# A fused RWKV-7 and Conformer layer: loads of the Pool queue held back and spread over slots, first loads in the order of use, the bonus loaded at once behind the recurrence

## The chip, the cores and the metric

The kernel runs on one core of one Trainium2 chip. The metric is device time in microseconds of one execution, from the first to the last instruction with what lies around it; three runs of the kernel before took 1825.54, 1830.32 and 1831.36 us, median 1830.32 us. A second kind of number is the span of a profiled execution, from its first to its last instruction.

## The reference

One layer works on 256 tokens of width 4096. A pre-normed input goes through one input projection; its columns feed an RWKV-7 group (32 heads of 64) and a Conformer convolution group of 2048 channels; both are gated, joined, projected again, post-normed and added to the input. Cut to what matters here:

```python
h = rms_norm(x, norm_pre_g)
proj = einsum('btd,dc->btc', h, w_in)                 # 256 x 4096 x 14528
rwkv_in, g_rwkv, glu_v, glu_g, g_conv = split(proj)
xs = rwkv_in + (prev - rwkv_in) * mu_shift            # token shift
r, k, v, w_low, a_low = split(xs)
decay = exp(-exp(-softplus(-(w0 + tanh(w_low) @ w_lora_up)) - 0.5))
a = sigmoid(a0 + a_low @ a_lora_up)
kk = k * k_k; kk = kk / max(norm(kk), 1e-12)
k_h = k * (1 + (a - 1) * k_a)
# per head, S of 64 x 64, over 256 steps:
#   S = S diag(w_t) + (S (-kk_t)) (kk_t a_t)^T + v_t k_t^T ;  y_t = S r_t
y = rwkv7_recurrence(r, decay, k_h, v, kk, a)
y = group_norm(y) * lnx_g + lnx_b
bonus = sum(r * k_h * r_k, per head) * v
y_rwkv = (y + bonus) * silu(g_rwkv)
c = silu(layer_norm(causal_conv31(glu_v * sigmoid(glu_g)) + conv_b))
y_conv = (c @ w_pw2 + b_pw2) * silu(g_conv)
out = concat([y_rwkv, y_conv]) @ w_out                # 256 x 4096 x 4096
return x + rms_norm(out, norm_post_g)
```

## The kernel before

The three big products are cut into blocks of 512 columns and 128 rows of depth. Their weights come from HBM in tiles `wr` of two depth steps (512 KB), issued on the SP queue five tiles ahead (`load`, four buffers). ScalarE rounds each 128x512 half to a TensorE format (`wh`), VectorE writes the rest of the rounding (`wl`), and TensorE forms three products per half of the tokens: `wh,lh`, `wl,lh`, `wh,ll`. One depth step of one block is a slot; it is six matmuls of 512 columns. The loop over `slots` writes PE, DVE and ACT out by hand (`MANUAL`): in each slot the six matmuls, then `side.step()`, then the `wh` of four slots later (`HL`) and the `wl` of three slots later (`LL`). The first two blocks run interleaved.

All else is side work: generators in lanes, which `side.step()` moves on once per slot. A plain `yield` ends a lane's part of the slot; `yield 0` lets it go on as long as a running account of DVE and ACT work stays below that of PE. Since the three engines run in the order in which instructions were written, a side instruction that waits holds up the `wh`, `wl` or matmuls written behind it.

The side work that the change touches, for 8 units `u` of 4 heads, two quads `qd` of 4 units:

- `job_prep(u)` (lane 4) forms the operands of the recurrence in chunks of 32 steps: `c_ar`, `c_q`, `c_bkt`, `c_uv`, and stores them on the POOL queue into the DRAM tensor `rec_dr`; a part of `c_q` goes into `n_dr`, the bonus `c_bv` into `bv_dr`.
- `job_inv(pr)` (lane 3) inverts the triangular 32x32 matrices of two units: an identity is loaded into `t_x` (line 595), `n_dr` is loaded four times into `c_y`, to 32 partitions each (line 600), and 31 steps of two DVE instructions follow, the first of which reads both (`c_sq<-t_x,c_y`).
- `job_chain(qd)` (lane 2) runs the recurrence over 8 chunks. `fetch(c)` loads one chunk's operands, 1 MB, from `rec_dr` into `c_st` (two buffers). At the end it norms the result and, per unit, loads the bonus into `t_x` (line 741), waits six slots and adds.

POOL and SP are not in `MANUAL`. A scheduler orders their DMA issues and may place an issue earlier than the code has it, as far as its tile is free and its source is written. Nothing else waits for an issue: it starts when the POOL queue comes to it.

At the start, `x_load(0)` loads the first four rows of tiles of the transposed input into `c_ar` and, between them, the first two weight halves; `load(1)` to `load(4)` follow. `WARM` matmuls on a zero tile run meanwhile.

Of the kernel before, what the change touches and what calls it, by code (L numbers as in the profile page):

```python
# [9 lines left out]
F32 = mybir.dt.float32  # L10
# [7 lines left out]
P = 128  # L18
# [6 lines left out]
CH = 32  # L25
NCH = T // CH
BN = 512
KC = 2
COL = dict(r=0, k=2048, v=4096, low=6144, g=6336, gv=8384, gg=10432, gc=12480)
PT = 2  # L30
RL0 = (BN + 2 * LORA) // 2
WARM = 9
SLACK = 0.0
CREDIT = 1500.0
HI_LEAD, LO_LEAD = 4, 3
# [142 lines left out]
def hybrid(ctx: ExitStack, tc, a, out):  # L178
# [108 lines left out]
    def x_load(i):  # L287
        if i < 4:
            st["xc"] = rw["pool"].tile([P, 4, T + 1], F32, name=XTAG[i], bufs=1)
        elif i % 2 == 0:  # L290
            st["xc"] = rw["pool"].tile([P, 8, T + 1], F32, name="c_st", bufs=2)
        o = 4 * (i % 2) if i > 3 else 0
        t = st["xc"][:, o:o + 4, :]
        if i == 0:
            for k0, k1 in ((0, 1), (1, 2), (2, 4)):
                nc.sync.dma_start(out=t[:, k0:k1, :], in_=xT_v[:, k0:k1, :])
                if k0 < KC:
                    load(0, k0)
        else:
            nc.sync.dma_start(out=t, in_=xT_v[:, 4 * i:4 * i + 4, :])  # L300
        st["xr", i] = t
# [98 lines left out]

    def c3(x):
        return x[:, 0:512].rearrange("p (c t) -> p c t", t=CH)

    def crossed(out, in_):

# [21 lines left out]
    def job_prep(u):  # L427
# [87 lines left out]
                scale=par("k_a", u * 2 + q), bias=oka[:, u * 2 + q:u * 2 + q + 1])  # L515
        vec.tensor_tensor(out=ar4[:, :, 0::3], in0=e2(c3(rs)), in1=e2(pt_[:, :, 1:C1]), op=ALU.mult)
        yield 0
        vec.tensor_tensor(out=kkn, in0=kkn, in1=av, op=ALU.mult)
        yield 0
        for q in range(2):  # L520
# [31 lines left out]
                                in_=qs[y * CH:(y + 1) * CH, :, 1 - x::2, x * CH:(x + 1) * CH])  # L552
        rw[("n", u)] = True
        for h in range(2):
            nc.gpsimd.dma_start(out=rec_dr[qd, :, :, un, 0, h * 64:h * 64 + 64].rearrange("c p x -> p c x"), in_=ar[:, h * 8:h * 8 + 8, :])  # L555
            nc.gpsimd.dma_start(out=rec_dr[qd, :, :, un, 1, h * 64:h * 64 + 64].rearrange("c p x -> p c x"), in_=qs[:, h])

        bp = yield from head_sums(bq, "t_sw")
# [30 lines left out]
    def job_inv(pr):  # L589

        rp = rw["pool"]
        while ("n", 2 * pr + 1) not in rw or (pr > 1 and not rw.get(("done", pr // 2 - 1))):
            yield "wait"
        xi = rp.tile([P, 2, 8, CH], F32, name="t_x", bufs=1)
        nc.gpsimd.dma_start(out=xi.rearrange("p n l k -> p (n l k)"), in_=a["cst"][:, CS["eye"][0]:CS["eye"][1]])
        yield
        yield
        nt = rp.tile([P, 2, CH, CH], F32, name="c_y", bufs=1)
        for rho in range(4):
            nc.gpsimd.dma_start(out=nt[rho * 32:(rho + 1) * 32].rearrange("p n k j -> p n (k j)"),  # L600
                                in_=n_dr[2 * pr:2 * pr + 2].rearrange("n y g k j -> (y g) n (k j)"))
        for _ in range(6):
            yield
        for k in range(CH - 1):

            l, m = k // 4 + 1, CH - 1 - k
            tm = rp.tile([P, 2, 8, CH], F32, name="c_sq", bufs=1)
            vec.tensor_tensor(out=tm[:, :, 0:l, 0:m], in0=xi[:, :, 0:l, k:k + 1].broadcast_to([P, 2, l, m]),
                              in1=nt[:, :, k:k + 1, k + 1:].broadcast_to([P, 2, l, m]), op=ALU.mult)
            yield 0  # L610
            vec.tensor_tensor(out=xi[:, :, 0:l, k + 1:], in0=xi[:, :, 0:l, k + 1:], in1=tm[:, :, 0:l, 0:m], op=ALU.subtract)
            yield 0
        yield
        xv = x_dr[2 * pr:2 * pr + 2].rearrange("n y g (l r) j -> r (y g) n l j", r=4)
        for rho in range(4):
            for un in range(2):
                nc.gpsimd.dma_start(out=xv[rho][:, un], in_=xi[rho * 32:(rho + 1) * 32, un])  # L617
        quad = rw["quad", pr // 2]
        if pr % 2 == 0:
            quad["x"] = rp.tile([P, 4, 8, CH], F32, name="c_x", bufs=1)  # L620
        xt = quad["x"][:, pr % 2 * 2:pr % 2 * 2 + 2]
        for y in range(4):
            for un in range(2):
                for h in range(2):
                    nc.gpsimd.dma_start(out=xt[y * CH:(y + 1) * CH, un, h * 4:h * 4 + 4],  # L625
                                        in_=x_dr[2 * pr + un, y ^ (2 * h), h * 4:h * 4 + 4].rearrange("g i j -> i g j"))
        for _ in range(15):
            yield
        if pr % 2:
            quad["xt"] = quad["x"]  # L630

    def job_chain(qd):
# [10 lines left out]
        UN = range(4)  # L643
        recs = {}

        def fetch(c):
            if c < NCH:
                recs[c] = rp.tile([P, 4, 4, 2, 64], F32, name="c_st", bufs=2)
                nc.gpsimd.dma_start(out=recs[c].rearrange("p n i h x -> p (n i h x)"), in_=rec_dr[qd, c].rearrange("p n i x -> p (n i x)"))

        def swap(x):
            return x.rearrange("p b n x -> p n b x")
# [1 line left out]
        def outputs(c):  # L654
            for rows in (slice(0, P),) if c % 2 == 0 else KS:
                vec.tensor_tensor(out=ys[rows, c // 2], in0=swap(pz[rows, :, :, RX]), in1=ry[rows], op=ALU.add)

        fetch(0)
        for _ in range(8):
            yield  # L660
        for c in range(NCH):
            vr, ur = VR[c % 2], UR[c % 2]
            fetch(c + 1)
            ar, qs, bkt, uv = (recs[c][:, :, i] for i in range(4))
            if c > 0:
                outputs(c - 1)
                Sn = rp.tile([P, 4, 2, 64], F32, name="c_s", bufs=2)
                dec = pc[:, :, c - 1::8].unsqueeze(3).broadcast_to([P, 4, 2, 64])
                if S is None:
                    vec.tensor_tensor(out=Sn, in0=swap(pz[:, :, :, RD]), in1=dec, op=ALU.mult)  # L670
                else:
                    vec.tensor_tensor(out=Sn, in0=swap(pz[:, :, :, RD]), in1=S, op=ALU.add)
                    vec.tensor_tensor(out=Sn, in0=Sn, in1=dec, op=ALU.mult)
                S = Sn
                yield
                yield
            pz = ps_ch.tile([P, 2, 4, P], F32, name="pz")

            for n in UN:
# [2 lines left out]
            for n in UN if S is not None else ():  # L682
                for q, h in DIAG:
                    pe.matmul(pz[HS[q ^ h], h, n, RX], ar[HS[h], n, q, :], S[HS[h], n, q, :], start=False, stop=n == 3)
            yield
            ry = rp.tile([P, 4, 2, 64], F32, name="t_x", bufs=1)
            act(out=ry, in_=swap(pz[:, :, :, RX]), func=AF.Copy)
# [15 lines left out]
                    pe.matmul(pz[ro[q ^ h], h, n, RX], qs[ur[q], n, h, k0:], uv[ur[q], n, h, :], start=True, stop=True)  # L703
            yield
        outputs(NCH - 1)
        yield 0

        mv = rp.tile([P, 2, 32], F32, name="c_mv", bufs=1)
# [28 lines left out]
        yield  # L737
        for n in UN:
            u = 4 * qd + n
            bv = rp.tile([P, 512], F32, name="t_x", bufs=1)  # L740
            nc.gpsimd.dma_start(out=bv, in_=bv_dr[u])
            for _ in range(6):
                yield
            yo = rp.tile([P, 16, CH], F32, name="c_sq", bufs=1)
            bv3 = bv.rearrange("p (c t) -> p c t", t=CH)
            yield from tp_wait()
            t = tp_get([P, 4, P])
            for i in range(4):
# [425 lines left out]
    HL, LL, RL = HI_LEAD, LO_LEAD, 5  # L1174
    with tc.manual_schedule(engines=MANUAL):
        x_load(0)
        load(1)
        warm = ptp.tile([P, 512], mybir.dt.bfloat16, name="pt")
        vec.memset(warm, 0.0)
        vec.memset(eps[:, 0:1], 1e-6)  # L1180
# [107 lines left out]
```

## Time and profile before

| | us |
|---|---|
| median of three runs | 1830.32 |
| the profiled execution's own time | 1828.64 |
| its span | 1826.7 |
| PE busy | 1808.9 |
| DVE busy | 1330.4 |
| ACT busy | 1008.8 |
| POOL busy | 195.7 |

The profiled execution is 1.68 us under the median, and 1.94 us of its time lie outside the span. Busy time of PE counts each matmul to its end; as matmuls overlap, a pace is better read from starts: one start to the next. A wait is idle time of an engine before an instruction, with what ended it. The names of waits are the tiles written, as in `PE acc`; L92 is a helper through which most instructions are recorded, so tiles, not lines, tell them apart.

### The profile page before, as it was taken

Reading aid. Unit: us, or ns where it says so; the run is one execution under the profiler, and the core shown is the slowest. Engines: PE = TensorE matmul, PEld = TensorE weight load, DVE = VectorE, ACT = ScalarE, POOL = GpSimd, SP = SyncE. Lnnn points to the kernel's source line nnn. Section 1 sums busy time; section 2 is a strip of 40 time slices with the busy share of each in tenths; the row PEclk is TensorE's granted clock in tenths of the full one; section 3 lists DMA queues with packets and bytes.
Section 4 is the critical chain, followed back from the end, with each engine's and each line's share of the span. In section 5 each row is a group of like instructions: output and inputs, shape, how many; then the busy total and the mean of one; then the engine's idle time right before and its main releaser. Section 6 shows DMA issues by size and latency. Waiting matters only on the chain.

```text
span 1826.7 us, 30061 instructions
## 1 busy us (share of the span) xinstructions
PE 1808.9 (99%) x10897; PEld 1492.1 (82%) x10897; DVE 1330.4 (73%) x2560; ACT 1008.8 (55%) x1729; POOL 195.7 (11%) x330
## 2 busy tenths in 40 slices
PE   9999999999999999999999999999999999999997
PEld 7899888888878877888888787778888888888886
DVE  6655778997779967899987898566677655555555
ACT  6756665556645455655566544445566444554453
POOL 0000112201022002030310220000100000000000
PEclk9999999999999999999999999999999999999999
DMA  9867678777787667687777877667877666666665
GB/s 332 272 175 202 205 213 241 206 209 206 221 268 211 188 215 227 197 254 236 202 221 216 282 226 225 221 198 212 270 241 255 241 195 199 198 196 199 201 200 189
DMA packets 202820, 404.88 MB, mean 222 GB/s; under 512 B 16176, under 2 KB 33712, under 8 KB 200368
## 3 DMA queue, kind: packets, MB, share of 16 engines
q1 hardware_dynamic: 182352, 335.31, 60.4%
q0 software_dynamic: 20320, 67.65, 11.7%
q8 instruction: 85, 1.39, 0.3%
q14 instruction: 63, 0.52, 0.1%
HBM read 371.45 MB, written 31.46 MB: 221 GB/s over the span
## 4 chain that ended last, share of the span: by engine, by line
PE 91%; DMA 4%; DVE 2%; issue 2%; POOL 1%; ACT 1%; DVEq 0%; SPq 0%; POOLq 0%; ACTq 0%
PE acc L92 85%; PE tp L92 3%; PE pz L92 3%; DMA c_y<-n_dr 1%; DMA wr<-in_w_in 1%; DVE wl L92 1%; DMA n_dr<-c_q 1%; DVE t L92 0%; DVE chl L92 0%; POOL n_dr L551 0%; POOL c_y L600 0%; DVE cw L92 0%; POOL rec_dr L555 0%; ACT wh L92 0%; ACT L92 0%
## 5 line engine op out<-in xcount | busy, mean ns | idle before, releaser
L92 ACT ACTIVATE wh<-wr 128x512 fp32r<-128x512 f32 (+1 forms) x1243 | 767.5, 624 | 671.4 <-PE acc L92 393.9
L92 DVE TENSOR_TENSOR wl<-wr,wh 128x512 fp32r<-128x512 f32 (+1 forms) x1243 | 830.0, 677 | 336.9 <-ACT wh L92 328.5
L92 PE MATMUL acc<-wh,lh 128*128 128x512 f32 (+1 forms) x2358 | 923.1, 391 | 1.4 <-ACT wh L92 1.4
L92 PE MATMUL acc<-wl,lh 128*128 128x512 f32 (+1 forms) x2358 | 911.3, 386 | 3.5 <-DVE wl L92 3.5
L92 PE MATMUL acc<-wh,ll 128*128 128x512 f32 (+1 forms) x2358 | 911.5, 387 | 0.0
L92 PEld LDWEIGHTS acc<-wl,lh 128*128 128x128 f32 x2358 | 443.6, 188 | 89.5 <-DVE wl L92 5.7
L92 PEld LDWEIGHTS acc<-wh,lh 128*128 128x128 f32 x2358 | 443.1, 188 | 90.0 <-ACT wh L92 2.7
L92 PEld LDWEIGHTS acc<-wh,ll 128*128 128x128 f32 x2358 | 443.0, 188 | 88.4
L92 DVE SCALAR_TENSOR_TENSOR cw<-up,pv,cw 128x256 f32<-128x256 f32 x480 | 217.4, 477 | 0.1
L92 PE MATMUL acc<-wh,chl 128*128 128x512 f32 x256 | 82.4, 397 | 0.0
L92 PEld LDWEIGHTS acc<-wh,chl 128*128 128x128 f32 x256 | 48.2, 188 | 10.9
L92 PE MATMUL acc<-wl,chl 128*128 128x512 f32 x128 | 50.5, 394 | 0.0
L555 POOL DMA_DIRECT2D rec_dr<-c_ar x16 | 14.3, 901 | 284.2 <-DVE c_ar L92 241.6
L92 DVE TENSOR_TENSOR c_sq<-t_x,c_y 128x120 f32<-128x120 f32 (+24 forms) x124 | 31.7, 256 | 14.7 <-DMA c_y<-n_dr 14.7
L92 ACT ACT_TABLE_LOAD x32 | 41.1, 1283 | 1.3 <-PEq L1257 0.7
L1029 POOL DMA_DIRECT2D bb<-in_norm_post_g x8 | 4.3, 538 | 303.3 <-DVE chl L92 258.9
L625 POOL DMA_DIRECT2D c_x<-x_dr x64 | 34.7, 551 | 12.9 <-DMA x_dr<-t_x 11.4
L92 PEld LDWEIGHTS pz<-c_st 32*64 32x64 f32 (+2 forms) x1472 | 25.0, 128 | 12.1 <-PE acc L92 4.6
L92 ACT ACTIVATE pt<-acc,rstd 128x512 f32<-128x512 f32 (+3 forms) x52 | 33.8, 655 | 1.1 <-PE acc L92 0.5
L92 DVE TENSOR_SCALAR c_st<-pz 32x512 f32<-32x512 f32 x16 | 11.1, 693 | 29.5 <-ACT c_st L92 29.5
L92 DVE TENSOR_TENSOR t_x<-t_x,c_sq 128x120 f32<-128x120 f32 (+24 forms) x124 | 31.6, 255 | 0.0
L617 POOL DMA_DIRECT2D x_dr<-t_x x32 | 18.5, 655 | 119.8 <-DVE t_x L92 119.3
(181 smaller groups left out, 933.9 us busy)
## 6 DMA issues: line engine op xcount, KB each, us to landing
wr<-in_w_in SPq DMA_DIRECT2D x431, 512.0 KB, 4.4
wr<-in_w_out SPq DMA_DIRECT2D x128, 512.0 KB, 4.5
c_st<-rec_dr POOLq DMA_DIRECT2D x16, 1024.0 KB, 6.6
wr<-in_w_pw SPq DMA_DIRECT2D x32, 512.0 KB, 4.5
wr<-in_w_in SPq DMA_DIRECT2D x16, 352.0 KB, 3.3
rec_dr<-c_ar POOLq DMA_DIRECT2D x16, 256.0 KB, 5.5
rec_dr<-c_q POOLq DMA_DIRECT2D x16, 256.0 KB, 4.2
rec_dr<-c_bkt POOLq DMA_DIRECT2D x8, 512.0 KB, 6.1
```

The costliest lines, as they stand in the source:

```text
L92: return f(*args, **kw)
L555: nc.gpsimd.dma_start(out=rec_dr[qd, :, :, un, 0, h * 64:h * 64 + 64].rearrange("c p x -> p c x"), in_=ar[:, h * 8:h * 8 + 8, :])
L617: nc.gpsimd.dma_start(out=xv[rho][:, un], in_=xi[rho * 32:(rho + 1) * 32, un])
L625: nc.gpsimd.dma_start(out=xt[y * CH:(y + 1) * CH, un, h * 4:h * 4 + 4], in_=x_dr[2 * pr + un, y ^ (2 * h), h * 4:h * 4 + 4].rearrange("g i ...
L1029: nc.gpsimd.dma_start(out=gb, in_=a["norm_post_g"][0:1, j * BN:(j + 1) * BN].broadcast_to([P, BN]))
```

## The change

It has five parts.

1. A helper `hold(t)` writes one column of a tile on DVE ahead of a load into it. The load must then wait for that DVE instruction, so that it can't start before DVE comes to that place.
2. `job_inv`: the identity is held; the four loads of `c_y` are held each and stand one slot apart. From its start to the first DVE step there are 17 slots, 8 before.
3. `job_chain`: a chunk's load is cut in two halves of 512 KB, each held, and written one and two slots into the chunk before; those of chunk 0 stand two slots apart ahead of the recurrence, which has 17 slots ahead of it, 8 before. The four bonus loads of a quad are written together behind the recurrence, into a buffer of `c_st`; the four times six slots of waiting go.
4. `job_prep`: the store of `c_ar` is written right behind its computation.
5. The start: the first part of the input goes out on the ACT queue, the other loads on SP in the order of use, with the first two weight tiles in four halves; `WARM` is 8 in place of 9.

```diff
@@ -29,7 +29,7 @@
 COL = dict(r=0, k=2048, v=4096, low=6144, g=6336, gv=8384, gg=10432, gc=12480)
 PT = 2
 RL0 = (BN + 2 * LORA) // 2
-WARM = 9
+WARM = 8
 SLACK = 0.0
 CREDIT = 1500.0
 HI_LEAD, LO_LEAD = 4, 3
@@ -292,10 +292,13 @@
         o = 4 * (i % 2) if i > 3 else 0
         t = st["xc"][:, o:o + 4, :]
         if i == 0:
-            for k0, k1 in ((0, 1), (1, 2), (2, 4)):
-                nc.sync.dma_start(out=t[:, k0:k1, :], in_=xT_v[:, k0:k1, :])
-                if k0 < KC:
-                    load(0, k0)
+
+            for k in range(KC):
+                (nc.sync if k else nc.scalar).dma_start(out=t[:, k, :], in_=xT_v[:, k, :])
+                load(0, k)
+            for k in range(KC):
+                load(1, k)
+            nc.sync.dma_start(out=t[:, KC:4, :], in_=xT_v[:, KC:4, :])
         else:
             nc.sync.dma_start(out=t, in_=xT_v[:, 4 * i:4 * i + 4, :])
         st["xr", i] = t
@@ -400,6 +403,10 @@
 
     def c3(x):
         return x[:, 0:512].rearrange("p (c t) -> p c t", t=CH)
+
+    def hold(t):
+
+        vec.memset(t, 0.0)
 
     def crossed(out, in_):
 
@@ -515,6 +522,8 @@
                 scale=par("k_a", u * 2 + q), bias=oka[:, u * 2 + q:u * 2 + q + 1])
         vec.tensor_tensor(out=ar4[:, :, 0::3], in0=e2(c3(rs)), in1=e2(pt_[:, :, 1:C1]), op=ALU.mult)
         yield 0
+        for q in range(2):
+            nc.gpsimd.dma_start(out=rec_dr[qd, :, :, un, 0, q * 64:q * 64 + 64].rearrange("c p x -> p c x"), in_=ar[:, q * 8:q * 8 + 8, :])
         vec.tensor_tensor(out=kkn, in0=kkn, in1=av, op=ALU.mult)
         yield 0
         for q in range(2):
@@ -552,7 +561,6 @@
                                 in_=qs[y * CH:(y + 1) * CH, :, 1 - x::2, x * CH:(x + 1) * CH])
         rw[("n", u)] = True
         for h in range(2):
-            nc.gpsimd.dma_start(out=rec_dr[qd, :, :, un, 0, h * 64:h * 64 + 64].rearrange("c p x -> p c x"), in_=ar[:, h * 8:h * 8 + 8, :])
             nc.gpsimd.dma_start(out=rec_dr[qd, :, :, un, 1, h * 64:h * 64 + 64].rearrange("c p x -> p c x"), in_=qs[:, h])
 
         bp = yield from head_sums(bq, "t_sw")
@@ -592,11 +600,14 @@
         while ("n", 2 * pr + 1) not in rw or (pr > 1 and not rw.get(("done", pr // 2 - 1))):
             yield "wait"
         xi = rp.tile([P, 2, 8, CH], F32, name="t_x", bufs=1)
+        hold(xi[:, 0, 0, 0:1])
         nc.gpsimd.dma_start(out=xi.rearrange("p n l k -> p (n l k)"), in_=a["cst"][:, CS["eye"][0]:CS["eye"][1]])
-        yield
-        yield
+        for _ in range(7):
+            yield
         nt = rp.tile([P, 2, CH, CH], F32, name="c_y", bufs=1)
         for rho in range(4):
+            yield
+            hold(nt[rho * 32:(rho + 1) * 32, 0, 0, 0:1])
             nc.gpsimd.dma_start(out=nt[rho * 32:(rho + 1) * 32].rearrange("p n k j -> p n (k j)"),
                                 in_=n_dr[2 * pr:2 * pr + 2].rearrange("n y g k j -> (y g) n (k j)"))
         for _ in range(6):
@@ -643,10 +654,14 @@
         UN = range(4)
         recs = {}
 
-        def fetch(c):
+        def fetch(c, half):
+
             if c < NCH:
-                recs[c] = rp.tile([P, 4, 4, 2, 64], F32, name="c_st", bufs=2)
-                nc.gpsimd.dma_start(out=recs[c].rearrange("p n i h x -> p (n i h x)"), in_=rec_dr[qd, c].rearrange("p n i x -> p (n i x)"))
+                if half == 0:
+                    recs[c] = rp.tile([P, 4, 4, 2, 64], F32, name="c_st", bufs=2)
+                un = slice(2 * half, 2 * half + 2)
+                hold(recs[c][:, 2 * half, 0, 0, 0:1])
+                nc.gpsimd.dma_start(out=recs[c][:, un].rearrange("p n i h x -> p (n i h x)"), in_=rec_dr[qd, c, :, un].rearrange("p n i x -> p (n i x)"))
 
         def swap(x):
             return x.rearrange("p b n x -> p n b x")
@@ -655,12 +670,16 @@
             for rows in (slice(0, P),) if c % 2 == 0 else KS:
                 vec.tensor_tensor(out=ys[rows, c // 2], in0=swap(pz[rows, :, :, RX]), in1=ry[rows], op=ALU.add)
 
-        fetch(0)
         for _ in range(8):
+            yield
+        for half in range(2):
+            fetch(0, half)
+            yield
+            yield
+        for _ in range(5):
             yield
         for c in range(NCH):
             vr, ur = VR[c % 2], UR[c % 2]
-            fetch(c + 1)
             ar, qs, bkt, uv = (recs[c][:, :, i] for i in range(4))
             if c > 0:
                 outputs(c - 1)
@@ -673,7 +692,11 @@
                     vec.tensor_tensor(out=Sn, in0=Sn, in1=dec, op=ALU.mult)
                 S = Sn
                 yield
+                fetch(c + 1, 0)
                 yield
+                fetch(c + 1, 1)
+            else:
+                fetch(1, 0)
             pz = ps_ch.tile([P, 2, 4, P], F32, name="pz")
 
             for n in UN:
@@ -682,6 +705,8 @@
             for n in UN if S is not None else ():
                 for q, h in DIAG:
                     pe.matmul(pz[HS[q ^ h], h, n, RX], ar[HS[h], n, q, :], S[HS[h], n, q, :], start=False, stop=n == 3)
+            if c == 0:
+                fetch(1, 1)
             yield
             ry = rp.tile([P, 4, 2, 64], F32, name="t_x", bufs=1)
             act(out=ry, in_=swap(pz[:, :, :, RX]), func=AF.Copy)
@@ -703,6 +728,9 @@
                     pe.matmul(pz[ro[q ^ h], h, n, RX], qs[ur[q], n, h, k0:], uv[ur[q], n, h, :], start=True, stop=True)
             yield
         outputs(NCH - 1)
+        bvs = rp.tile([P, 4, 512], F32, name="c_st", bufs=2)
+        for n in UN:
+            nc.gpsimd.dma_start(out=bvs[:, n], in_=bv_dr[4 * qd + n])
         yield 0
 
         mv = rp.tile([P, 2, 32], F32, name="c_mv", bufs=1)
@@ -737,12 +765,8 @@
         yield
         for n in UN:
             u = 4 * qd + n
-            bv = rp.tile([P, 512], F32, name="t_x", bufs=1)
-            nc.gpsimd.dma_start(out=bv, in_=bv_dr[u])
-            for _ in range(6):
-                yield
             yo = rp.tile([P, 16, CH], F32, name="c_sq", bufs=1)
-            bv3 = bv.rearrange("p (c t) -> p c t", t=CH)
+            bv3 = bvs[:, n].rearrange("p (c t) -> p c t", t=CH)
             yield from tp_wait()
             t = tp_get([P, 4, P])
             for i in range(4):
@@ -1174,7 +1198,6 @@
     HL, LL, RL = HI_LEAD, LO_LEAD, 5
     with tc.manual_schedule(engines=MANUAL):
         x_load(0)
-        load(1)
         warm = ptp.tile([P, 512], mybir.dt.bfloat16, name="pt")
         vec.memset(warm, 0.0)
         vec.memset(eps[:, 0:1], 1e-6)
```

What the scheduler makes of it on the POOL queue is shown first at the start of the program. Names are the tiles written and read; 128x512 is partitions by elements. Before:

```order
L1263 UNCONDITIONAL_BRANCH
L595 DMA t_x<-in_cst 128x512
L430 DMA t_bk<-in_w_lora_up 96x256
L431 DMA t_bk<-in_a_lora_up 96x256
L555 DMA rec_dr<-c_ar 128x8x64 x2
```

And of the change, at the same place:

```order
L1286 UNCONDITIONAL_BRANCH
L437 DMA t_bk<-in_w_lora_up 96x256
L438 DMA t_bk<-in_a_lora_up 96x256
L526 DMA rec_dr<-c_ar 128x8x64 x2
L564 DMA rec_dr<-c_q 128x8x64
```

The identity's load for the first inversion no longer stands at the start; it now stands behind the stores of the second unit. `rec_dr<-c_ar` stands where it stood, ahead of `c_q`.

The second place on POOL is from the fourth unit's stores to the first chunks of the recurrence. Before:

```order
L551 DMA n_dr<-c_q 32x8x32 x4
L556 DMA rec_dr<-c_q 128x8x64
L600 DMA c_y<-n_dr 32x2x1024 x4
L406 DMA bv_dr<-c_bv 64x512
L408 DMA bv_dr<-c_bv 64x256 x2
L585 DMA rec_dr<-c_bkt 128x8x128
L585 DMA rec_dr<-c_uv 128x8x128
L430 DMA t_bk<-in_w_lora_up 96x256
L431 DMA t_bk<-in_a_lora_up 96x256
L649 DMA c_st<-rec_dr 128x2048 x2
L617 DMA x_dr<-t_x 256x1x32 x8
```

And of the change:

```order
L604 DMA t_x<-in_cst 128x512
L413 DMA bv_dr<-c_bv 64x512
L415 DMA bv_dr<-c_bv 64x256 x2
L593 DMA rec_dr<-c_bkt 128x8x128
L611 DMA c_y<-n_dr 32x2x1024
L593 DMA rec_dr<-c_uv 128x8x128
L611 DMA c_y<-n_dr 32x2x1024 x3
L437 DMA t_bk<-in_w_lora_up 96x256
L438 DMA t_bk<-in_a_lora_up 96x256
L820 DMA c_dr<-cw 128x512
L628 DMA x_dr<-t_x 256x1x32 x8
L636 DMA c_x<-x_dr 32x4x32 x16
```

The four loads of `c_y` now stand behind the bonus and `c_bkt` stores, three of them behind `c_uv` too, and two lora loads stand behind them; the two 1 MB chunk loads that stood ahead of the inversion's end are gone from here (they follow, in halves, behind the last row shown).

The third place is DVE at the first inversion. `cw` is convolution work, `s_k` the shift of another projection. Before:

```order
L92 TENSOR_TENSOR c_bv<-tp,s_v 128x512
L92 SCALAR_TENSOR_TENSOR cw<-up,pv,cw 128x256
L92 TENSOR_TENSOR wl<-wr,wh 128x512
L92 SCALAR_TENSOR_TENSOR cw<-up,pv,cw 128x256 x2
L92 TENSOR_TENSOR wl<-wr,wh 128x512
L92 SCALAR_TENSOR_TENSOR cw<-up,pv,cw 128x256 x2
L92 TENSOR_TENSOR wl<-wr,wh 128x512
L92 SCALAR_TENSOR_TENSOR cw<-up,pv,cw 128x256 x2
L92 TENSOR_TENSOR wl<-wr,wh 128x512
L92 SCALAR_TENSOR_TENSOR cw<-up,pv,cw 128x256 x2
L92 TENSOR_TENSOR wl<-wr,wh 128x512
L92 TENSOR_TENSOR c_sq<-t_x,c_y 128x2x31
```

And of the change, where five slots of convolution work like those above stand between `c_bv` and the first row here, and four more such slots between the last row here and `c_sq<-t_x,c_y`:

```order
L92 MEMSET c_y 32x1
L92 SCALAR_TENSOR_TENSOR cw<-up,pv,cw 128x256 x2
L92 TENSOR_TENSOR wl<-wr,wh 128x512
L92 MEMSET c_y 32x1
L92 SCALAR_TENSOR_TENSOR cw<-up,pv,cw 128x256 x2
L92 TENSOR_TENSOR wl<-wr,wh 128x512
L92 MEMSET c_y 32x1
L92 SCALAR_TENSOR_TENSOR cw<-up,pv,cw 128x256
L92 TENSOR_TENSOR wl<-wr,wh 128x512
L92 MEMSET c_y 32x1
L92 SCALAR_TENSOR_TENSOR cw<-up,pv,cw 128x256 x2
L92 TENSOR_TENSOR wl<-wr,wh 128x512
```

The step that reads `c_y` moved nine slots back, from the 223rd `wl` of the program to the 232nd, in all four inversions alike; the last `MEMSET` of `c_y` stands six slots ahead of it.

## Rows read from the trace of the kernel before

**Rows 1.** The page: span, and busy us (share), instructions of each engine.

```profile
span 1826.7 us, 30061 instructions
PE 1808.9 (99%) x10897; PEld 1492.1 (82%) x10897; DVE 1330.4 (73%) x2560; ACT 1008.8 (55%) x1729; POOL 195.7 (11%) x330
```

**Rows 2.** Waits of PE: engine, tile, releaser: us in total, times, longest.

```profile
PE acc L92 <- DVE wl L92: 3.5, 4, 1.7
PE tp L92 <- ACT pt L92: 1.5, 1, 1.5
PE acc L92 <- ACT wh L92: 1.4, 2, 0.8
```

**Rows 3.** Windows of PE: stretch, us, PE busy (x), clock, DMA share, GB/s.

```profile
5.86:9.60 3.74, 3.74 (x8) 1.00 1.04 385
540.00:544.00 4.00, 2.48 (x14) 1.00 1.01 381
1500.00:1600.00 100.00, 100.00 (x443) 1.00 0.67 199
```

**Rows 4.** Timeline of PE: start, us, instruction, [idle before <-releaser].

```profile
298.84 0.39 PE L92 MATMUL acc<-wh,lh 128*128 128x512 f32 x1
300.02 0.50 PE L92 MATMUL acc<-wl,lh 128*128 128x512 f32 x1 [0.80 <-DVE wl L92]
...
525.00 0.39 PE L92 MATMUL acc<-wh,lh 128*128 128x512 f32 x1
527.06 0.50 PE L92 MATMUL acc<-wl,lh 128*128 128x512 f32 x1 [1.68 <-DVE wl L92]
...
541.93 0.27 PE L92 MATMUL tp<-cst,pt 128*128 128x128 f32 x1
543.72 0.55 PE L92 MATMUL tp<-cst,pt 128*128 128x128 f32 x3 [1.52 <-ACT pt L92]
...
1043.75 0.39 PE L92 MATMUL acc<-wh,ll 128*128 128x512 f32 x1
...
1045.64 0.50 PE L92 MATMUL acc<-wl,lh 128*128 128x512 f32 x1 [0.23 <-DVE wl L92]
```

**Rows 5.** Waits of DVE.

```profile
DVE c_sq L92 <- DMA c_y<-n_dr: 14.7, 4, 4.9
```

**Rows 6.** Tile `c_y`, POOL, from 280 to 1030 us: 16 loads.

```profile
DMA to landing us min/median/max: 4.7/7.6/9.0
```

**Rows 7.** Timeline of POOL, 505 to 546 us.

```profile
530.60 1.10 POOL L649 DMA_DIRECT2D c_st<-rec_dr  x2 [6.18 <-DMA wr<-in_w_in]
```

**Rows 8.** DMA issues from 530 to 535 us: count, KB each, median us to landing.

```profile
c_st<-rec_dr POOLq DMA_DIRECT2D x2, 1024.0 KB, 9.7
wr<-in_w_in SPq DMA_DIRECT2D x2, 512.0 KB, 9.6
```

**Rows 9.** Timeline of ACT, 523 to 546 us.

```profile
542.46 0.63 ACT L92 ACTIVATE wh<-wr 128x512 fp32r<-128x512 f32 x1 [5.77 <-DMA wr<-in_w_in]
```

**Rows 10.** Tile `c_st`, from 1110 to 1220 us: six chunk loads.

```profile
DMA to landing us min/median/max: 5.2/6.3/6.8
```

**Rows 11.** DMA issues from 600 to 712 us.

```profile
wr<-in_w_in SPq DMA_DIRECT2D x31, 512.0 KB, 4.0
```

**Rows 12.** Tile `eps`: duration min/median/max in ns.

```profile
L92 DVE MEMSET eps<- x3: 59/59/59, 1.1 to 1.1; 128x1 f32 x3
```

**Rows 13.** Timeline of the first 6 us.

```profile
1.18 0.42 SPq L1131 DMA_DIRECT2D wr<-in_w_in  x1
1.19 4.02 PE L1186 MATMUL tp<-pt 128*128 128x512 bf16 x9 [1.19 <-DVE eps L92]
1.25 0.67 POOL L595 DMA_DIRECT2D t_x<-in_cst  x1 [0.81 <-POOLq L1257]
...
5.17 0.63 ACT L92 ACTIVATE wh<-wr 128x512 fp32r<-128x512 f32 x1 [1.72 <-DMA wr<-in_w_in]
...
5.86 0.79 PE L92 MATMUL acc<-wh,lh 128*128 128x512 f32 x1 [0.65 <-ACT wh L92]
```

## The prediction

> **What bounds the kernel now.** I read the page first. PE is busy for 1808.9 of 1826.7 us [rows 1], so all but 17.8 us of the span lie under matmuls, and work taken off other engines is worth nothing by itself. Busy time overstates what PE does, as one matmul overlaps the next, so I looked at the pace: between 1500 and 1600 us, in the last product, 443 matmuls of 512 columns start in 100 us, 0.226 us each, without a gap [rows 3]. The big products are all matmuls of that kind, and nothing in the change makes one shorter. What can be gained are places where PE falls off the pace, and the start.
>
> PE waits seven times for ACT's and DVE's work, 6.4 us in all [rows 2]; one of the seven, 0.65 us, is the first big matmul's, and the other six lie at five places. The timeline of PE shows what each costs from start to start, which is more than the idle time [rows 4]. At 298.84 us the next matmul starts 1.18 us later, not 0.23: 0.95 us lost, and 0.1 us more at the slow restart, 1.05. The same picture stands once more, at 1026.54, another 1.05. At 525.00 it is 2.06 - 0.23 + 0.1 = 1.93. At 541.93 a transpose waits: 1.79 us to the next start where 0.11 is usual, 1.68. At 1043.75 two matmuls take 1.89 where two need 0.45: 1.44. The five sum to 7.15 us.
>
> They have two causes. DVE waits four times for `c_y`, 14.7 us in all [rows 5]: the first step of each inversion stands in DVE's order ahead of the next `wl`, and the loads of `c_y` land up to 9.0 us after their issue [rows 6]. Three of the four reach PE, as 1.05, 1.93 and 1.05; the longest, 4.9 us, as 1.93. So what ScalarE and VectorE have prepared covers about 3 us. The two others are late weights. At 530.60 POOL issues two chunk loads of 1 MB back to back [rows 7], before the recurrence needs either; they take 9.7 us, and the weight tiles issued meanwhile 9.6 us [rows 8], where 4.0 is usual beside single chunk loads [rows 11]. DMA then moves 381 GB/s at a full share, against 199 in quiet stretches [rows 3]; ACT sits 5.77 us for a weight tile [rows 9], and PE loses 1.68. At 1032 us the second quad does the same, for 1.44.
>
> **The change part by part.** *Inversions.* In place of 8 slots there are 17 from the start to the first step. A slot is at least 6 x 0.226 = 1.36 us. The last of the four loads is held to six slots ahead of its reader, 8.2 us. Four issued together landed within 4.7 to 9.0 us, the first of a burst soonest [rows 6]. One per slot is 256 KB in 1.36 us, 193 GB/s, beside 193 GB/s of weights: 386, just what DMA moved at its fullest [rows 3], so the last load is behind a short queue. I take 6 us and a reader that waits for nothing; from the other side 9.0 + 0.3 for the hold, 1.1 us late, still inside the 3 us that are covered. So the 1.05 + 1.93 + 1.05 = 4.03 us go. What is late next is nothing on PE: the inversion ends nine slots later, but the recurrence behind it stood idle for a while, and its matmuls only move.
>
> *Chunk loads.* The first chunk comes in two halves two slots apart and is held to the slots just ahead of its use, so two 1 MB loads no longer meet. Their 3.12 us go. The nearest row for what replaces them is the single 1 MB load in the recurrence: 5.2 to 6.8 us [rows 10], without a late weight on PE there. Two new waits are possible, and both would stop PE itself, since the chunk's matmuls stand in its order. Chunk 0's second half is issued six slots, 8.2 us, before its first matmul; half of 6.8 us or the 4.0 of a 512 KB weight tile are the nearest, so it is in time. Chunk 1 comes as both halves in the slot of chunk 0's matmuls, with the same six slots: 6.8, 0.3 allowed for the hold and 0.55 for the second issue (rows 7 have 1.10 for two) are 7.7 us, 0.5 in hand. From chunk 2 on the second half has at least seven slots, 9.5 us. I put 0.4 us on chunk 1 of both quads together; the ends are 0 and 2 x (9.7 + 0.9 - 8.2) = 4.8, if they are as slow as the colliding pair.
>
> The row gives a size for the cut into halves; the Trainium skill speaks against it. Its page "DMA: Bandwidth & Descriptors" (sections Bandwidth, and Anatomy of one DMA) asks for transfers of 1 MiB and more, and puts some 2 us of fixed cost on each issued from GpSimd. By that, an estimate, a chunk in halves is complete about 2 us later, chunk 1 is 1.5 us late in either quad, and the sum falls by 3 us. The rows have 512 KB in 4.0 us [rows 11], which shows both halves under way at once to be no slower, and the sum goes by them.
>
> *Holds.* There are 5 x 4 for the inversions and 16 x 2 for the chunks, 52 DVE writes of one column, 59 ns each [rows 12]: 3.1 us on an engine that is 73% busy [rows 1]. Spread over 1248 slots they hide under matmuls. Behind a hold DVE queues only if its tile is still being read; each chunk's hold stands behind DVE's own reading of the last result of that buffer, so it has no wait of its own. POOL's queue does wait at a hold, and behind it stand stores and the lora loads of the next unit, which are read dozens of slots later. Cost nothing; 1 us if DVE runs full where holds and unit 4's or 5's preparation meet, as both now overlap the first recurrence.
>
> *Slots of the chain.* 9 more in the inversion and 9 more ahead of chunk 0 against 24 fewer at its end: each quad is done 6 slots sooner after its last unit's store. PE never waits for it, so that is nothing, either way. The bonus loads, 4 x 256 KB at once, are one burst of 1 MB like those of rows 10 and are read some 20 slots later. The store of `c_ar` stands on POOL where it stood: nothing.
>
> *The start.* The first weight half was issued at 1.18 us and was there at 5.17, 3.99 us later [rows 13]. It is now SP's first issue, one issue of 0.42 us sooner. The identity's 256 KB, which POOL issued at 1.25 us into the same stretch, are gone from it, 0.68 us at the 385 GB/s of rows 3. The first matmul comes 0.4 to 1.1 us sooner, 0.7 in the middle; the nine warm matmuls end at 5.2 [rows 13], eight near 4.8, so the hole between them and the first big one stays as it is. But PE runs its first 3.74 us at the half clock: 8 matmuls, 0.47 us each [rows 3], which is the pace of 1.2 GHz though the clock column has 1.00. If the clock rises at the same moment as before, the earlier start is worth half, 0.35; with the rise as long behind the first matmul as before, 0.7. I take 0.5. The bounds: with no half-clock stretch at all 0.7 + 3.74 / 2 = 2.6 gained; with such a stretch twice as long 1.9 - 0.4 = 1.5 lost. The ACT queue's first use for a load is not in the trace; ScalarE, done with the input part that it will carry, sat 1.72 us until the first weight came [rows 13], so that load can be 0.6 us slower for nothing even if the weight comes 1.1 us sooner.
>
> *Sum.* 4.0 + 3.1 + 0.5 - 0.4 = 7.2 us. From the profiled execution's 1828.64 us that is 1821.4. That execution lies 1.7 us under the median of the three runs, so the same sum from the median is 1823.1. I say 1822.
>
> **The rivals.** *The stalls go in part.* Loads that were early now come just in time: if DVE still waits 4 us at an inversion, or the weights are late behind four `c_y` loads, a `c_uv` store and two lora loads in eight slots, half of the 7.1 comes back: 1822 + 3.6 = 1825.6. For it: DMA at a full share wherever POOL loads meet weights. Against: before, the four loads met the same stores in one burst, and the weights were late only when 2 MB of chunks met.
>
> *Chunk 1 alone is late.* Each quad loses the upper bound above: 1822 + 4.8 - 0.4 = 1826.4. For it: chunk 1 has the least slack of all, 0.5 us. Against: rows 10. The skill's page named above, with its fixed cost on each half, points the same way, and no row here has it.
>
> *Chunks come late, and it is slower.* The place is PE's first matmul of chunks 1 to 7 in both quads, 14 of them; a chunk has seven slots, 9.5 us, from its second half's issue, and less for chunk 1. From the point where halves land later than that each microsecond counts 14 times. At the 9.7 us of rows 8 with 0.9 for hold and issues it is 1.1 x 14 = 15 us: 1822 + 15 = 1837. For it: loads held back have no slack to give. Against: none of the six took over 6.8 us [rows 10].
>
> *Nothing is gained.* The start loses 1.5 us where 0.5 was counted as won, and some 4.5 of the freed stalls reappear where DVE now has holds, recurrence and preparation in the same slots: 1822 + 2.0 + 4.5 = 1828.5. For it: each stall here is short, and PE's lead of 3 us is used up wherever DVE runs full.
>
> **How the numbers follow.** A measurement of this kernel can tell about 0.3%, 5.5 us, from no change. The forecast, 1822, has 0.58; from either base it is past that bound by 1 to 3 us. In part, 1825.6: 0.18. Chunk 1 late, 1826.4: 0.04. Nothing, 1828.5: 0.12. These three are within the bound. Chunks late, 1837: 0.08. That gives faster 0.58, same 0.34, slower 0.08. The likeliest one's own range is 1817 (the start's 2.6 and the slow restarts in full, runs 2 us under) to 1825. The range for 8 in 10 reaches into the second case: 1816 to 1828.
>
> **What would show it.** PE's waits on `wl` and `wh` near 300, 525, 542, 1026 and 1044 us are gone, and the waits of DVE have no `c_y`, or under 3 us at a time. Chunk loads of 512 KB land within 7 us, no weight tile takes over 8, and PE has no wait at the first matmul of a chunk. The first big matmul starts near 5.2 us. It would be wrong if PE's waits name `c_st` or DVE at `MEMSET`, if weight tiles are late in new places, or if the half-clock pace reaches past 9.6 us.

## The result: slower, and the profile after

The changed kernel takes 1837.95 us, median of six runs (1834.56 to 1840.24); the kernel before, on the same chips, 1827.96 (six runs, the three known ones among them). The ratio is 1.0052, 95% interval 1.0038 to 1.0066. I had forecast 1822. The profiled execution took 1838.57 us.

The page of the changed kernel, in the form of [rows 1], and the chunk loads' row of its DMA issues:

```profile
span 1836.8 us, 30167 instructions
PE 1812.1 (99%) x10896; PEld 1493.9 (81%) x10896; DVE 1333.0 (73%) x2612; ACT 1010.0 (55%) x1729; POOL 204.0 (11%) x346
...
c_st<-rec_dr POOLq DMA_DIRECT2D x32, 512.0 KB, 6.7
```

The span grew by 10.1 us, PE's busy time by 3.2. The waits of PE and, below them, two of DVE's in the changed kernel (engine, tile, releaser: us in total, times, longest), which answer to [rows 2] and [rows 5]:

```profile
PE acc L92 <- DVE wl L92: 7.6, 5, 3.0
PE tp L92 <- DVE c_sq L92: 4.3, 2, 2.3
...
PE tp L92 <- ACT t L92: 0.7, 1, 0.7
PE acc L92 <- ACT wh L92: 0.6, 1, 0.6
```

```profile
DVE c_sq L92 <- DMA y_dr<-c_sq: 22.3, 6, 4.5
DVE c_sq L92 <- DMA c_y<-n_dr: 4.5, 2, 3.7
```

The waits on `c_y` fell from 14.7 to 4.5 us; I had forecast none, or under 3 us at a time, and one of the two left is 3.7. The first row of DVE is new: six waits for a store. Both names begin with `c_sq`, but it is another use of that tile: here DVE writes a unit's output into it, in the tail of the recurrence.

To see where time came from I set the two traces side by side by counting the matmuls of the big products, six to a slot. By slot 1 the changed kernel is 1.5 us ahead, by slot 543 (789 us after, 794 before) 5.3 us. Between slots 551 and 564, the tail of the first quad's recurrence, it goes from 7.5 ahead to 0.7 behind. At slot 861, where the second quad's tail begins, it is 1.05 ahead, at slot 874 10.6 behind, and it ends 10.2 behind. All else that the change did is, taken together, a gain; two short stretches lost it.

The timeline of DVE in the second of them (start, us, instruction, idle before and releaser):

```profile
1276.10 0.88 DVE L92 SCALAR_TENSOR_TENSOR c_sq<-tp,pv,c_st 128x256 f32<-128x256 f32 x2 [1.25 <-PE tp L92]
1276.89 0.68 DVE L92 TENSOR_TENSOR wl<-wr,wh 128x512 fp32r<-128x512 f32 x1
1282.03 0.88 DVE L92 SCALAR_TENSOR_TENSOR c_sq<-tp,pv,c_st 128x256 f32<-128x256 f32 x2 [4.46 <-DMA y_dr<-c_sq]
1282.82 0.68 DVE L92 TENSOR_TENSOR wl<-wr,wh 128x512 fp32r<-128x512 f32 x1
1287.35 0.88 DVE L92 SCALAR_TENSOR_TENSOR c_sq<-tp,pv,c_st 128x256 f32<-128x256 f32 x2 [3.84 <-DMA y_dr<-c_sq]
1288.14 0.68 DVE L92 TENSOR_TENSOR wl<-wr,wh 128x512 fp32r<-128x512 f32 x1
1293.26 0.88 DVE L92 SCALAR_TENSOR_TENSOR c_sq<-tp,pv,c_st 128x256 f32<-128x256 f32 x2 [4.44 <-DMA y_dr<-c_sq]
```

Four units' outputs follow each other, one `wl` apart. `c_sq` is one buffer. Each unit's write waits until the store of the unit before has landed, which is issued by POOL and takes up to 4 us; DVE does one `wl` in 5 to 6 us where PE needs one every 1.37. From POOL's timeline the last of the three issues of the first unit's store and the first of the second's, and the landing of all in that stretch:

```profile
1277.92 0.52 POOL L415 DMA_DIRECT2D y_dr<-c_sq  x1
1282.81 0.52 POOL L415 DMA_DIRECT2D y_dr<-c_sq  x1 [4.36 <-DVE c_sq L92]
```

```profile
DMA to landing us min/median/max: 1.9/3.2/4.0
```

PE in the same stretch, its waits alone:

```profile
1283.05 0.63 PE L92 MATMUL tp<-cst,c_y 128*128 128x128 f32 x4 [1.94 <-DVE c_sq L92]
1288.88 0.79 PE L92 MATMUL acc<-wl,lh 128*128 128x512 f32 x1 [2.20 <-DVE wl L92]
1294.79 0.50 PE L92 MATMUL acc<-wl,lh 128*128 128x512 f32 x1 [2.99 <-DVE wl L92]
```

Before, each unit loaded its bonus and let six slots pass, 8.2 us: long enough for the load, and for the store that nobody had named. The change took the six slots with the load.

### The profile page after: what moved, and what is told of

Same layout as the page of the kernel before. It is cut to its first block, busy times and chain, and to the rows that moved or that the text cites. A ratio compares the mean times of both kernels' runs of the same rounds, so it can differ in the third digit from the quotient of the medians.

```text
span 1836.8 us, 30167 instructions
## 1 busy us (share of the span) xinstructions
PE 1812.1 (99%) x10896; PEld 1493.9 (81%) x10896; DVE 1333.0 (73%) x2612; ACT 1010.0 (55%) x1729; POOL 204.0 (11%) x346
## 3 DMA queue, kind: packets, MB, share of 16 engines
q0 software_dynamic: 22624, 67.66, 11.8%
q8 instruction: 85, 1.39, 0.3%
## 4 chain that ended last, share of the span: by engine, by line
PE 95%; DMA 2%; DVE 1%; issue 1%; POOL 1%; ACT 0%; DVEq 0%; POOLq 0%; ACTq 0%
PE acc L92 89%; PE tp L92 3%; PE pz L92 3%; DMA y_dr<-c_sq 1%; DMA c_y<-n_dr 1%; DMA t_bk<-in_a_lora_up 0%; DVE cw L92 0%; DVE wl L92 0%; DVE chl L92 0%; DMA c_ar<-in_xT 0%; POOL y_dr L415 0%; DVE c_sq L92 0%; POOL y_dr L413 0%; POOL c_y L611 0%; DVE c_bv L92 0%
## 5 line engine op out<-in xcount | busy, mean ns | idle before, releaser
L92 PEld LDWEIGHTS acc<-wl,lh 128*128 128x128 f32 x2358 | 444.3, 188 | 93.6 <-DVE wl L92 10.1
L664 POOL DMA_DIRECT2D c_st<-rec_dr x32 | 17.0, 535 | 161.4 <-DVE c_st L92 88.1
```

Of the source, the lines that this page charges most:

```text
L92: return f(*args, **kw)
L664: nc.gpsimd.dma_start(out=recs[c][:, un].rearrange("p n i h x -> p (n i h x)"), in_=rec_dr[qd, c, :, un].rearrange("p n i x -> p (n i x)"))
```

## The experiments

Twelve kernels ran. Each time stands beside the kernel before on the same chip (medians 1828.3 to 1829.0).

**Six slots put back** into the changed kernel, its bonus loads left together:

```diff
             u = 4 * qd + n
+            for _ in range(6):
+                yield
             yo = rp.tile([P, 16, CH], F32, name="c_sq", bufs=1)
```

> The changed kernel with six slots of waiting put back ahead of each unit's output in the tail of the recurrence; the four bonus loads stay together. Theory S (store): c_sq has one buffer, and the six slots covered the landing of the store of the unit before (4 us). Then DVE's waits on y_dr go (22.3 us to under 1), and with them the 7.0 us that PE loses from 798 to 830 us and the 11.4 us from 1268 to 1299 us: 1838 - 18 = 1820 us, within 3. Rival L (loads): the four bonus loads at once and the recurrence moved 22 slots crowd the DMA queues; nothing of that changes here, so 1838, within 2.

Measured: 1844.31 us, ratio 1.0091 (1.0076 to 1.0106), worse still. The waits on `y_dr` are gone from DVE's list, as the store theory says. But two others came; the waits of PE, and the cause of the first among the waits of ACT from 955 to 985 us:

```profile
PE tp L92 <- ACT t L92: 6.5, 1, 6.5
PE acc L92 <- ACT chl L92: 5.9, 3, 3.8
PE acc L92 <- DVE chl L92: 4.0, 3, 1.7
```

```profile
ACT t L92 <- DMA t_bk<-in_a_lora_up: 10.6, 1, 10.6
```

`chl` is the normed convolution, the operand of the second product. The layer norm may start only when the second quad's recurrence is done, because its tiles take that memory. The change adds nine slots in the inversions and nine ahead of chunk 0; with the tail at its old length the norm's second mean stands at slot 915, 22 later than before, and the product catches up with it: from slot 920 to 942 this run loses 17.6 us against before (two of the expectations below take 16). In the changed kernel the mean stands at slot 888: the 24 slots taken from the tail had paid for what the other parts added. The other wait is a lora load that the scheduler put on POOL behind 24 transfers of an inversion's result (`x_dr`, `c_x`), at 970.92 us instead of 964.38 in the changed kernel. So my theory was right on the store and had missed what the slots were for.

**Four output buffers** in the tail, no slot put back; the free buffer of `c_st` holds them:

```diff
+        yos = rp.tile([P, 4, 16, CH], F32, name="c_st", bufs=2)
...
-            yo = rp.tile([P, 16, CH], F32, name="c_sq", bufs=1)
+            yo = yos[:, n]
```

> The changed kernel with four output buffers for the tail of the recurrence (the second buffer of c_st, free by then) in place of one c_sq; no slot is put back. Theory S: no write waits for a store, 1820 us within 3, as with the slots. Rival W (work): it is the shorter tail, four units' transposes and DVE work in a few slots, that PE and DVE can't take; then the waits on y_dr go but PE still loses most of the 18 us in these stretches: 1832 to 1838.

Measured: 1822.38 us, 0.9970 (0.9958 to 0.9982): faster than before, and 15.6 us under the changed kernel. By slot it parts from the changed kernel in the two tails, by 6.3 and 10.8 us, and by 0.3 us elsewhere; the spans are 17.4 us apart, the medians 15.6. Work was not too dense; the one buffer was the whole loss. What PE still waits for:

```profile
PE tp L92 <- ACT t L92: 0.6, 1, 0.6
PE acc L92 <- ACT wh L92: 0.6, 1, 0.6
PE acc L92 <- DVE wl L92: 0.2, 1, 0.2
PE tp L92 <- DVE t L92: 0.2, 1, 0.2
```

**The bonus part alone** on the kernel before (part 3's last sentence in the list of the change, nothing else of it).

> The kernel before with the bonus part alone: four loads together behind the recurrence, no slots of waiting. Theory S: three waits of some 4 us per quad on y_dr, six in all, and a loss near the 18 us of the changed kernel: 1828 + 14 to 20 = 1842 to 1848. Rival L or a mere meeting of the parts: without held loads and a moved recurrence the tail alone costs little, 1828 to 1832.

Measured: 1846.79 us, 1.0103 (1.0088 to 1.0118). It loses as forecast, with no held load and no moved recurrence; two of its waits of DVE:

```profile
DVE c_sq L92 <- DMA y_dr<-c_sq: 18.0, 5, 4.5
DVE c_sq L92 <- DMA c_y<-n_dr: 17.5, 4, 5.3
```

**The start alone** (part 5).

> The kernel before with the start alone: first input part on the ACT queue, loads in the order of use, eight warm matmuls. In the trace of the changed kernel PE is 1.5 us ahead by the second slot. If that is the start's own: 1828 - 1.5 = 1826.5. If it is due to the identity's load that a hold keeps out of the first microseconds, it is smaller here: first big matmul at 5.4 us or later, and the half-clock pace back, 1827.5.

Measured: 1827.51 us, 0.9995 (0.9986 to 1.0005): no difference that can be measured. In its trace it is 1.3 us ahead by slot 1 and ends 1.2 ahead; the first big matmul starts at 5.57 us, as in the second theory, but the full pace is there from 6.6 us, so most of the 1.5 us is the start's own in this trace.

**The inversions alone** (part 2 with `hold`), and **the same without holds**:

> The kernel before with the inversions' part alone: holds, loads of c_y one slot apart, 17 slots in place of 8. The layer norm's second mean stands at slot 903 of the matmul order (893 before, 915 in the run with six slots back, where PE lost 16 us waiting for its result). Theory: DVE's waits on c_y go or stay under 4 us and reach PE with under 1 us, a gain of 3 to 4: 1828.4 - 3.5 = 1825. If ten slots of the norm's slack already cost: PE waits on chl, 1828 or more.

> As the inversions alone, but without the holds: the same 17 slots, the loads go out as soon as the queue can. If the slots give the gain: DVE has no wait on c_y at all (loads land 9 us after issue, the first step is some 12 us later than before), 1825 or less. If the holds and the spreading give it, by keeping four loads from meeting: DVE's waits stay over 2 us and the time is 1827 to 1829.

Measured: 1836.74 us, 1.0044 (1.0029 to 1.0059), and 1837.49 us, 1.0053 (1.0037 to 1.0070). Both lose, where I expected a gain. The waits on `c_y` went in both, from 14.7 to 2.0 and 0.4 us, so the slots do that and not the holds. But the norm comes at slots 903 and 904, and that is late already; the waits of PE in the first of the two:

```profile
PE tp L92 <- ACT t L92: 2.6, 1, 2.6
...
PE acc L92 <- ACT chl L92: 2.0, 1, 2.0
PE acc L92 <- DVE chl L92: 1.7, 1, 1.7
```

Set beside before by slots, the first is 2.4 us behind at slot 925 and 8.1 at slot 942: 5.7 us for ten slots of delay, which I had counted as slack. The wait for `t` is a late lora load again.

**The chunks alone** (part 3 without the bonus).

> The kernel before with the chunks' part alone: halves, held, 17 slots ahead of the recurrence. Theory: the late weight tiles near 542 and 1044 us go, no PE wait names a chunk: 1828.4 - 3.1 = 1825.3. Rival: halves that come just in time stop PE at the first matmul of a chunk, above all of chunk 1: 1828 to 1835, with waits of PE on c_st.

Measured: 1827.80 us, 0.9994 (0.9984 to 1.0003), inconclusive by time. The trace has no late weight near 542 or 1044 us any more and no PE wait for a chunk. By slot it gains 1.75 and 1.57 us at these two places, where I had counted 1.68 and 1.44. But the nine slots ahead of chunk 0 bring the norm to slot 902: PE waits 1.8 us for `chl`, and the run goes from 4.5 us ahead at slot 931 to 0.5 at slot 942. So the deadline took that gain back. Halves, holds and moved slots were not run apart, and the earlier store of `c_ar` (part 4) has no run of its own.

**Three slots put back** into the changed kernel.

> The changed kernel with three slots put back per unit of the tail, half of what was taken. Store theory: two units are then some 4 slots, 5.5 us, apart, more than the 4 us to a store's landing and less than 3 us of PE's cover short of it: waits on y_dr under 1 us each. The norm's second mean stands at slot 900, ahead of the run where it was late (915): no PE wait on chl. Together 1820 to 1823. If the tail needs all six slots: 1828 or more.

Measured: 1822.68 us, 0.9964 (0.9951 to 0.9977). Between the two losses lies room: one wait on `y_dr` is left, 1.4 us where I had said under 1, and one on `chl`, 0.6 where I had said none.

**The end 18 slots later**, the kernel before with nothing else:

```diff
+        for _ in range(18 * qd):
+            yield
         for n in UN:
             u = 4 * qd + n
```

> The kernel before with nothing but 18 slots of waiting added ahead of the output part of the second quad's tail, so that the recurrence's end and the layer norm behind it come 18 slots later (second mean at slot 911; 893 before, 915 with six slots back). Deadline theory: the second product can't start on the normed tiles in time; PE waits on chl, and the loss is near that of the run with six slots back, less four slots of 1.37 us: 16 - 5 = 11, so 1839 to 1840. Rival: that run lost by its POOL order or its holds; then here 1828 to 1830.

Measured: 1841.41 us, 1.0073 (1.0055 to 1.0092). The deadline by itself, with no hold and no load moved, costs 13.1 us: it is 1.1 ahead at slot 931 and 11.8 behind at 942. Its waits of PE:

```profile
PE acc L92 <- ACT chl L92: 5.3, 2, 3.8
PE acc L92 <- DVE chl L92: 3.3, 2, 1.7
```

**The tail with four buffers alone** on the kernel before.

> The kernel before with the bonus part alone, but four output buffers. No wait on y_dr, and the end comes 24 slots sooner. If a sooner end is worth something by itself: 1826 or less. If it only pays for slots added elsewhere: the five stalls of before stay, 1828 to 1829.

Measured: 1829.41 us, 1.0007 (0.9997 to 1.0018). An end 24 slots sooner is worth nothing until something else needs them.

**Inversions with that tail.**

> The inversions' part with the tail of four output buffers, on the kernel before. Alone the inversions' part took 1836.7: its gain on c_y went to the late norm. With the 24 slots given back the norm is early: the gain of 4 us stands, 1824 to 1825, and the weight stalls near 542 and 1044 us (3 us) stay. If the loss of the inversions alone had another cause: 1830 or more.

Measured: 1824.93 us, 0.9983 (0.9973 to 0.9992). The inversions alone lost 7.7 us; with the norm early they gain 3.3. PE has no wait on `chl`, and none for the late `t` either; the run does not part the two.

**All parts, four output buffers, no holds in the inversions.**

```diff
-        hold(xi[:, 0, 0, 0:1])
...
-            hold(nt[rho * 32:(rho + 1) * 32, 0, 0, 0:1])
```

> The changed kernel with four output buffers and without the holds of the inversions (their 17 slots stay). If the holds are worth nothing there, as the two runs of the inversions alone say: 1822 within 1, DVE's waits on c_y under 0.5 us. If an unheld identity in the first microseconds or four loads that meet cost: 1823.5 or more.

Measured: 1820.27 us, 0.9959 (0.9946 to 0.9973), the fastest here and faster than either kernel. It lies below the 1822 within 1 of the first theory. Whether it beats the version with those holds (1822.38) is open: the two intervals overlap. What its DVE waits for on `c_y` (1.4 us where I had said under 0.5) and what PE waits for in the big products:

```profile
DVE c_sq L92 <- DMA c_y<-n_dr: 1.4, 1, 1.4
```

```profile
PE acc L92 <- ACT wh L92: 0.6, 1, 0.6
PE acc L92 <- ACT t L92: 0.3, 1, 0.3
```

## Why the prediction was wrong

**The step that failed** is *Slots of the chain*: "9 more in the inversion and 9 more ahead of chunk 0 against 24 fewer at its end", and "PE never waits for it, so that is nothing, either way". The term was put at nothing, and it cost the whole loss: the 24 slots were not only a wait for the bonus, they also covered the store of the unit before, which frees the single `c_sq`. Without them PE loses 17.4 us by the traces, 15.6 by the medians, against four buffers; the bonus part alone loses 18.4, and with four buffers 1.2. "Either way" is wrong as well, though that cost nothing in the changed kernel, whose norm comes five slots sooner than before (888 against 893): the end of the recurrence is a deadline; 18 slots later cost 13 us, some ten cost 5.7. I had counted the slots right, and asked only whether PE waits for the recurrence's result, not which buffers the waiting had covered nor who takes over the memory. None of the four rivals was this one. "Chunks come late" had 1837, within 1 us of the measured time, but another mechanism, so it came close by luck: its place was PE's first matmul of a chunk, and PE has no wait there.

**Inversions, 4.0 us.** Right in mechanism and nearly in size: 3.3 us measured where nothing is late behind them, and by slot the changed kernel gains 1.1, 2.0 and 1.1 us where I had 1.05, 1.93 and 1.05. Wrong in a term: the loads of `c_y` took up to 11.6 us, where I took 6 and at most 9.3:

```profile
DMA to landing us min/median/max: 5.5/8.5/11.6
```

The last lands too late by 3.7 us in the second inversion, which PE's cover left at 0.5 from start to start (0.38 idle, at 535 us). I had said that PE's waits "near 300, 525, 542, 1026 and 1044 us are gone"; they are, that one small wait apart. The second and third row here show two of the five stretches in the changed kernel, and the first row the start (compare [rows 3]: there 540 to 544 had 2.48 us busy at 381 GB/s):

```profile
5.36:9.10 3.74, 3.55 (x14) 1.00 1.03 386
524.00:528.00 4.00, 4.00 (x20) 1.00 1.04 286
540.00:544.00 4.00, 4.00 (x21) 1.00 0.61 173
```

**Chunk loads, 3.1 us less 0.4.** The weight stalls went and no PE wait names a chunk, so the slower rival was wrong. But a half took 5.0 to 9.9 us to land in the second quad (twelve of its halves), median 6.9, against 6.3 for a whole chunk [rows 10]:

```profile
DMA to landing us min/median/max: 5.0/6.9/9.9
```

From the first half's issue to the second's landing chunks 1 to 7 of both quads take 8.4 us in the median, some 2 us more than whole ones; 0.5 us of that is the second issue, since POOL mostly issues the second half right behind the first and not a slot later. The Trainium skill's page "DMA: Bandwidth & Descriptors" (Anatomy of one DMA) states a fixed cost of some 2 us for each transfer issued from GpSimd, and I had set it aside on a row of weight tiles from another queue. The median, 8.4 us against 6.3, agrees with the estimate made from it; chunk 1, which that estimate had 1.5 us late, took 5.4 and 7.3 us and was not late. No run here separates that cost from the other transfers in these slots.

It cost nothing on PE, because there was more room than I gave: from the second half's issue to the chunk's first matmul 13.3 to 16.3 us passed, where I had counted 8.2 for chunk 1 and 9.5 for the others. Two second halves took 9.8 and 9.9 us to land, past what I had counted.

**Holds, nothing.** Right: 52 writes, and DVE's busy time grew by 2.6 us. In the inversions they bring no gain that the runs show; those of the chunks were never taken out alone.

**The start, 0.5 us.** 1.5 us ahead at slot 1 in the changed kernel, 1.3 alone, more than I took and within the bounds; by time it can't be told from nothing. The first big matmul came at 5.36 us, and the third starts 0.22 us before the next, at the full clock, where before [rows 3] eight matmuls had taken 3.74 us:

```profile
5.36 0.54 PE L92 MATMUL acc<-wh,lh 128*128 128x512 f32 x1 [0.58 <-ACT wh L92]
6.09 0.50 PE L92 MATMUL acc<-wl,lh 128*128 128x512 f32 x1 [0.18 <-DVE wl L92]
6.43 0.39 PE L92 MATMUL acc<-wh,ll 128*128 128x512 f32 x1
6.65 0.39 PE L92 MATMUL acc<-wh,lh 128*128 128x512 f32 x1
```

**The sum.** 7.2 us forecast without the tail; the run with four buffers, which has every part but that loss, ends 7.2 us ahead of before in its trace and 6.1 in the medians. That the trace meets the forecast to the tenth is luck: by slot that run gains 1.8 us at the start, 4.2 at three inversions and 2.9 at the two late weights, 8.9 together, and loses 1.7 us in other places, which no run here separates. The changed kernel is that run and the tail's loss. The 17.4 us are the difference of these two spans (1836.8 and 1819.4), but two other runs give the same: the bonus part alone with one buffer and with four, 1846.79 - 1829.41 = 17.4.

## What to carry to other kernels

A wait that looks like one load's may cover others: before taking it out, list every single-buffer tile written behind it and the store that must land first. A side job's length is free only up to its deadline, so look for who takes over its memory, and not only for who reads its result. Parts of a change can pay for each other: here the inversions' slots alone cost 8 us, and with the tail shortened they gain 3.

## What the runs showed that I had not expected

PE's waits can also cost the clock. In the changed kernel's second tail PE sits idle for 1.9, 2.2 and 3.0 us within 14 us; the windows of PE in that stretch (us, PE busy and matmuls, granted clock, DMA share, GB/s), and one microsecond of the third by itself:

```profile
1282.00:1288.00 6.00, 3.62 (x17) 1.00 0.20 46
1288.00:1294.00 6.00, 2.93 (x6) 0.72 0.46 131
1294.00:1299.00 5.00, 4.21 (x12) 0.67 0.67 182
1299.00:1304.00 5.00, 5.00 (x24) 0.99 0.99 340
1296.00:1297.00 1.00, 1.00 (x4) 0.50 0.89 150
```

The granted clock falls to its lower level, 1.2 GHz (0.50 in the last row), for part of 1288 to 1299 us, and matmuls start 0.43 us apart where 0.23 is usual, PE having worked 3.62 of the six microseconds before. The first tail has 0.72 in the same way (822 to 828 us). Of the 17.4 us, PE's five waits in the two tails hold 11.3, and 18 starts 0.43 us apart instead of 0.23 make 3.6; I take the rest for slower restarts, which no run here separates.

After the single waits of 0.80, 1.68 and 1.52 us in [rows 4] the granted clock stayed at 1.00, and so it did after one of 1.99 us at 301 us in the run of the bonus part alone. But crowding is not needed. In the run with the end 18 slots later, a wait of 1.39 us, with 0.22 us more behind it, was followed by the lower level, PE having been busy for 5.35 of the six microseconds up to 1042 us:

```profile
1042.74 0.50 PE L92 MATMUL acc<-wh,lh 128*128 128x512 f32 x1 [1.39 <-ACT wh L92]
```

```profile
1045.00:1047.00 2.00, 2.00 (x6) 0.50 0.45 108
```

What decides between the two cases, no run here shows.

The start's clock differs from run to run of nearly the same code: with four buffers the full pace was there from the third big matmul on, at 6.4 us, in the version without inversion holds only from 10 us. The identity's load, which the latter has at 1.25 us, is not enough to explain it: the start alone has it there too. So a microsecond in the first ten of one trace proves little.
